# Squared-ReLU MLP of a hybrid decoder step on one core: four inner blocks per down pass, a folded output gate, and stored weight sums

## The chip, the cores and the metric

The kernel runs on one core of one Trainium2 chip. The metric is the device time of one execution in microseconds (us), and the median of the executions shown is what counts. The engines are TensorE (PE; its weight loads are listed as PEld), VectorE (DVE), ScalarE (ACT), GpSimd (POOL) and SyncE (SP), which issues nearly all DMAs.

## The reference, cut to what matters

One inference step of a one-layer decoder runs over 2048 prompt tokens and 32 sample tokens of width 1024: a Mamba-2 group and a sliding-window attention group side by side, an output projection with a residual LayerNorm, then a dense MLP. The change lies in the MLP alone:

```python
h = x * (1.0 + sc_f) + sh_f
u = jnp.square(jax.nn.relu(jnp.einsum('btd,df->btf', h, w_up)))      # 1024 -> 4096
f = jnp.einsum('btf,fd->btd', u, w_down)                            # 4096 -> 1024
x = layer_norm(ALPHA * x + g_f * f, ln2_g, ln2_b)                   # ALPHA = 2 ** 0.25
```

Here `x` is the output of the first LayerNorm, and `g_f` is a row of 1024 gates, one per output column, the same for all prompt tokens.

## The kernel before, in words

Everything is in fp32. A product of two fp32 matrices is made of three fp32r matmuls: each operand is split into a high part (`hi`, an ACT copy to fp32r) and a rest (`lo = src - hi`, a subtraction on DVE or POOL), and `mm3` (L174 to L177) adds hi·hi, hi·lo and lo·hi in PSUM. `split` (L170 to L172) is the helper that makes the two parts.

The MLP walks over the prompt in four quarters `q` of 512 tokens. In each quarter 16 steps `p` stream the same weights again, 256 of the 4096 inner columns at a time (two inner blocks of 128). A step has these parts:

- `w_up` (L1242) loads the 256 columns of w_up as two tiles of 512 KB, `wra` (two buffers) and `wrc` (one buffer), through the SP queue (L1164).
- `w_sums`, by way of `up_ops` (L1167 to L1182), makes the seven weight blocks of a Strassen-Winograd product: DVE forms four sums or differences of half tiles (L1175 `ws`, L1177 `wrc`, L1178 and L1179 `wra`), and the tiles are split into wA, w1, wB and wC. The `lo` parts of wA and wC are made on POOL, those of w1 and wB on DVE (all L1172). These split tiles have one buffer each.
- `up` (L1311) makes seven products of 12 matmuls, each 256 tokens wide (272 in the last quarter, which takes the sample tokens along), in three PSUM tiles `sc`. DVE adds them up straight from PSUM (L1325), squares the ReLU in SBUF (L1339), ACT copies the high part of u (L1341), POOL makes its low part (L1345).
- `w_down` (L1250) loads one block of 128 rows of w_down (`p6` or `p7`, 512 KB, L1252), DVE multiplies it by the gate row into `st2` (L1255, listed as `st<-p,ho`), and `split` gives `wdh` (ACT, L171) and `wdl` (POOL, L172). There are three buffers of each.
- `down` (L1351) runs two such blocks against the two u blocks: for four token tiles `j` and two column halves `n`, 6 matmuls of 512 columns into a PSUM tile (`mm`, three buffers, or `tr`, two). DVE then adds the PSUM tile to the accumulator of that token tile in SBUF (L1374, `p<-mm,p`), which makes 8 additions a step; in the first pass of a quarter ACT copies instead (L1372). The last pass of the last quarter already takes four blocks.

`slot()` (L1267) runs background jobs from a list `bg` at fixed points of a step. `residual(q)` (L1285) fills it: per quarter, rows alpha·ln1_g and alpha·ln1_b are fetched, and each of the four token tiles gets three DVE operations of 128x1024 (L1292 and L1293: xhat times the row, added to the accumulator; L1296: the second row added). At the end of a quarter `h_load` (L1304) fetches and splits the next 512 tokens of h, `finish` (L1403) normalizes, and the results are stored. The sample tokens' down product is kept in one PSUM tile `dec` through the last quarter from raw w_down blocks, and gets its gate and residual in `finish_dec`.

A scheduler orders the instructions of each engine when the program is built; on the chip each engine takes its list in order. SP's list is one queue too: a DMA that waits for its buffer holds back those behind it.

## Time and profile before

| | |
|---|---|
| median of 3 runs | 2650.69 us (2650.53 to 2659.85) |
| the profiled execution: its time | 2660.37 us |
| its span, first to last instruction | 2658.6 us |
| mean granted TensorE clock | 0.965 |
| matmuls / DVE / ACT / POOL instructions | 14231 / 3465 / 1751 / 705 |
| HBM read / written | 253.81 MB / 53.02 MB |

The profiled execution is 9.7 us (0.4%) above the median. The MLP takes the stretch from 967 to 2649 us of the span. A row of a group reads: line, engine, operation, tiles written and read, shapes and count, then busy time in us and mean ns of one, then the idle time of the engine just before those instructions and what ended it. PE's busy time is modelled, since matmuls are pipelined; the distance between the starts of two matmuls shows what one costs in a stream.

### The profile page before, as it was taken

What the parts mean: (1) busy time and instruction counts of PE and PEld (TensorE: products, weight loads), DVE (VectorE), ACT (ScalarE), POOL (GpSimd) and SP (SyncE); (2) the same over time, 40 slices, a digit from 0 to 9 for tenths busy, and PEclk for the clock granted to TensorE, in tenths of its full rate; (3) what the DMA queues carried; (4) which work ended last, traced back from release to release, by engine and by line L of the source; (5) the groups of instructions that cost most, each with busy time, mean ns of one, the idle gap of its engine ahead of it and who ended that gap; (6) DMA issues with size and microseconds to landing.
All of it is one profiled execution on the core that took longest, in us unless ns stands there. A gap on an engine that the chain in (4) does not pass through costs nothing. (4 is left out here: it accounts for less than half of the span.)

```text
span 2658.6 us, 37118 instructions
## 1 busy us (share of the span) xinstructions
PE 2396.3 (90%) x14231; PEld 2015.6 (76%) x14231; DVE 2250.1 (85%) x3465; ACT 958.7 (36%) x1751; POOL 1275.9 (48%) x705
## 2 busy tenths in 40 slices
PE   7899989999999998889978889987889987889997
PEld 5567769878978877778867778876778876777885
DVE  6666677878888779998898998998998899899887
ACT  3544553324345343223234223233223333323332
POOL 4333421332232036556567555567555557546554
PEclk9899999999999999999989999998999998999999
DMA  8654423233154443322223322223332222323221
GB/s 316 235 196 140 132 98 106 62 113 98 60 181 153 172 178 116 107 102 91 94 87 127 111 95 96 88 95 105 102 107 91 96 80 80 119 90 102 80 76 61
DMA packets 111715, 308.23 MB, mean 116 GB/s; under 512 B 15713, under 2 KB 38705, under 8 KB 108385
## 3 DMA queue, kind: packets, MB, share of 16 engines
q1 hardware_dynamic: 106560, 293.78, 32.3%
q10 hardware_dynamic: 4976, 12.07, 1.2%
q8 instruction: 112, 1.84, 0.3%
q14 instruction: 67, 0.54, 0.1%
HBM read 253.81 MB, written 53.02 MB: 115 GB/s over the span
## 5 line engine op out<-in xcount | busy, mean ns | idle before, releaser
L172 POOL TENSOR_TENSOR wdl<-st,wdh 128x1024 fp32r<-128x1024 f32 x127 | 331.2, 2608 | 208.9 <-ACT wdh L171 197.0
L175 PE MATMUL sc<-Hh,wCh 128*128 128x256 f32 (+1 forms) x504 | 158.3, 314 | 127.2 <-DVE U L1325 98.0
L171 ACT ACTIVATE wdh<-st 128x1024 fp32r<-128x1024 f32 x127 | 134.1, 1056 | 293.3 <-DVE st L1255 234.7
L1172 POOL TENSOR_TENSOR wCl<-wrc,wCh 128x1024 fp32r<-128x1024 f32 x63 | 184.5, 2929 | 105.7 <-ACT wCh L1171 97.9
L1255 DVE TENSOR_TENSOR st<-p,ho 128x1024 f32<-128x1024 f32 x128 | 218.3, 1705 | 15.0 <-DMA p<-in_wd 10.4
L1374 DVE TENSOR_TENSOR p<-mm,p 128x512 f32<-128x512 f32 x328 | 217.5, 677 | 5.8 <-PE mm L177 5.8
L175 PEld LDWEIGHTS sc<-Hh,wCh 128*128 128x128 f32 x504 | 102.2, 203 | 153.5 <-DVE U L1325 121.2
L1172 POOL TENSOR_TENSOR wAl<-wra,wAh 128x1024 fp32r<-128x1024 f32 x63 | 166.8, 2648 | 65.5 <-ACT wAh L1171 65.5
L1345 POOL TENSOR_TENSOR B<-c,A 128x512 fp32r<-128x512 f32 x64 | 100.2, 1566 | 139.4 <-ACT A L1341 136.5
L1345 POOL TENSOR_TENSOR u<-c,x 128x512 fp32r<-128x512 f32 x64 | 101.3, 1583 | 134.6 <-ACT x L1341 134.6
L175 PE MATMUL sc<-Hh,wBh 128*128 128x256 f32 (+1 forms) x504 | 149.1, 296 | 16.9 <-DVE c L1325 11.3
L183 POOL TENSOR_TENSOR rs<-ve,mhalf 128x1 f32<-128x1 f32 (+2 forms) x68 | 49.8, 734 | 236.1 <-DVE ve L182 207.1
L175 PE MATMUL mm<-wdh,A 128*128 128x512 f32 x358 | 145.7, 410 | 14.9 <-DVE p L1374 14.7
L1171 ACT ACTIVATE wBh<-wra 128x1024 fp32r<-128x1024 f32 x63 | 66.9, 1061 | 243.0 <-DVE wra L1179 152.5
L1339 DVE SCALAR_TENSOR_TENSOR c<-c 128x512 f32<-128x512 f32 (+1 forms) x128 | 152.0, 1187 | 0.3
L177 PE MATMUL sc<-Hh,wCl 128*128 128x256 f32 (+1 forms) x504 | 150.5, 299 | 0.0
L176 PE MATMUL sc<-Hl,wCh 128*128 128x256 f32 (+1 forms) x504 | 150.4, 298 | 0.0
L177 PE MATMUL sc<-Hh,wBl 128*128 128x256 f32 (+1 forms) x504 | 145.5, 289 | 1.4 <-DVE wBl L1172 1.4
L175 PE MATMUL mm<-wdh,x 128*128 128x512 f32 x352 | 139.8, 403 | 7.8 <-DVE p L1374 7.6
L175 PE MATMUL sc<-Hh,wAh 128*128 128x256 f32 (+1 forms) x504 | 145.7, 289 | 0.8 <-DVE c L1325 0.7
L176 PE MATMUL sc<-Hl,wAh 128*128 128x256 f32 (+1 forms) x504 | 145.1, 288 | 0.4
L176 PE MATMUL sc<-Hl,wBh 128*128 128x256 f32 (+1 forms) x504 | 145.3, 288 | 0.0
(528 smaller groups left out, 8420.7 us busy)
## 6 DMA issues: line engine op xcount, KB each, us to landing
p<-in_wd SPq DMA_DIRECT2D x128, 512.0 KB
wra<-in_wu SPq DMA_DIRECT2D x63, 512.0 KB
...
```

The lines of the kernel that those rows point to most:

```text
L171: S.activation(hi, src, AF.Copy)
L172: (eng or V).tensor_tensor(lo, src, hi.bitcast(F32), ALU.subtract)
L175: PE.matmul(out, lhsT=ahi, rhs=bhi, start=first, stop=False)
L176: PE.matmul(out, lhsT=ahi, rhs=blo, start=False, stop=False)
L177: return PE.matmul(out, lhsT=alo, rhs=bhi, start=False, stop=last)
L183: G.tensor_tensor(r[:P], v[:P], mhalf[:P, 0:n], ALU.pow)
L1171: S.activation(w[0], t, AF.Copy)
L1172: eng.tensor_tensor(w[1], t, w[0].bitcast(F32), ALU.subtract)
L1255: V.tensor_tensor(s2, st, gf, ALU.mult)
L1339: V.scalar_tensor_tensor(c[i][:, :, :N], c[i][:, :, :N], 0.0, c[i][:, :, :N], ALU.max, ALU.mult)
L1345: G.tensor_tensor(h3_(ul), c[i][:, :, 0:256], h3_(uh).bitcast(F32), ALU.subtract)
L1374: V.tensor_tensor(a, mm, a, ALU.add)
```

## The change

The change does five things.

1. **Four blocks per down pass.** The loop is over 8 passes `d` per quarter: two up steps, four `w_down` blocks, one `down` with groups of 12 matmuls. `wdh` and `wdl` get four buffers each, exactly one pass. The accumulators get 8 additions per pass, so per two steps.
2. **The gate is folded into the accumulators.** w_down is split as it was loaded, from `p6`/`p7` themselves, without `st2`. After the seventh pass of a quarter the accumulators are multiplied by the gate row once (`fold`), and the four blocks of the last pass are still multiplied by the gate on DVE.
3. **Weight sums are stored.** In the first quarter the sums that `up_ops` makes are written to DRAM (`sum_d`); later quarters load them and skip the four DVE operations. They then load the first raw tile, three stored pieces and half of the second raw tile: five DMAs, 1.75 MB a step in place of two with 1 MB. Both `wra` buffers are used in every step.
4. **Residual rows are made ahead.** alpha·(xhat·ln1_g + ln1_b) of all 16 token tiles and the sample tokens is made in the background of the first three quarters, two DVE operations a tile, and stored in `xres_d`; `fold` loads it and adds it, one operation.
5. One of the seven up products takes an `mm` tile in place of an `sc` tile; the blocks of the last quarter are loaded into four buffers; the sample tokens' residual and gate are fetched in `finish_dec`.

```diff
+    xres_d = tc.dram_tile([NTOK, DM], F32, name="xres_d")
+    sum_d = tc.dram_tile([16, 128, 4, 512], F32, name="sum_d")
...
         put(wa, ra, G)
-        V.tensor_tensor(s1, rc[:, 0], rc[:, 1], ALU.add)
-        put(w1, s1, V)
-        V.tensor_tensor(rc[:, 0], ra[:, 0], rc[:, 0], ALU.subtract)
-        V.tensor_tensor(ra[:, 0], s1, ra[:, 0], ALU.subtract)
-        V.tensor_tensor(ra[:, 1], ra[:, 1], ra[:, 0], ALU.subtract)
+        if q:
+            ra, s1 = wup[p][2:]
+            put(w1, s1, V)
+        else:
+            V.tensor_tensor(s1, rc[:, 0], rc[:, 1], ALU.add)
+            put(w1, s1, V)
+            V.tensor_tensor(rc[:, 0], ra[:, 0], rc[:, 0], ALU.subtract)
+            V.tensor_tensor(ra[:, 0], s1, ra[:, 0], ALU.subtract)
+            V.tensor_tensor(ra[:, 1], ra[:, 1], ra[:, 0], ALU.subtract)
+            D.dma_start(out=sum_d[p][:, 0], in_=s1)
+            D.dma_start(out=sum_d[p][:, 1], in_=rc[:, 0])
+            D.dma_start(out=sum_d[p][:, 2:4], in_=ra)
         put(wb, ra, V)
         put(wc, rc, G)
...
-    def w_down(f, w=None):
-        st = prt(6 + f % 2)
+    def w_down(f, q, gf=None, w=None):
+        st = prt((6, 7, 4, 5)[f % 4] if q == 3 else 6 + f % 2)
         D.dma_start(out=st, in_=I["wd"][f])
-        hi, lo = w or [wt(1024, "wd" + c, 3) for c in "hl"]
-        s2 = wt(1024, "st2", 1, F32)
-        V.tensor_tensor(s2, st, gf, ALU.mult)
-        split(hi, lo, s2, G)
+        hi, lo = w or [wt(1024, "wd" + c, 4) for c in "hl"]
+        src = st
+        if gf is not None:
+            src = wt(1024, "wra", 2, F32) if q == 3 else st
+            V.tensor_tensor(src, st, gf, ALU.mult)
+        split(hi, lo, src, G)
         return hi, lo, st
...
+    def fold(q, j, gf):
+        r = spare(q, j % 2) if q < 3 else wt(1024, "wra", 2, F32)
+        D.dma_start(out=r, in_=xres_d[128 * tok(q, j):128 * tok(q, j) + 128])
+        V.tensor_tensor(acc[q, j], acc[q, j], gf, ALU.mult)
+        V.tensor_tensor(acc[q, j], acc[q, j], r, ALU.add)
...
-        p5 = prod(1)
+        p5 = prod(1, mm_tile)
...
+        for d in range(8):
+            us, ws = [], []
+            for i in range(2):
+                us.append(step(2 * d + i, q))
+                for f in range(4 * d + 2 * i, 4 * d + 2 * i + 2):
+                    ws.append(w_down(f, q, gf))
...
+            down(q, us, ws, d, dec)
...
+            if d == 6:
+                gf = ada_row(q2("ho"), 5, 128)
+                bg.extend([lambda q=q, j=j, gf=gf: fold(q, j, gf)] for j in range(4))
```

How the lists of the engines change is shown at three places. First DVE's list in a step of the MLP before: `ws`, `wrc` and `wra` (from L1175 and L1177 to L1179) are the weight sums, `st2` the gated block of w_down, `sc` the up products in PSUM, and `p2`, `p3` accumulators.

```order
L1175 TENSOR_TENSOR ws_12456<-wrc_12341 128x512
L1374 TENSOR_TENSOR p3_10276<-tr_12324,p3_10276 128x512
L1177 TENSOR_TENSOR wrc_12341<-wra_12340,wrc_12341 128x512
L1374 TENSOR_TENSOR p3_10276<-tr_12332,p3_10276 128x512
L1325 TENSOR_TENSOR U2_12345<-sc_12363,X1_12344 128x256
L1255 TENSOR_TENSOR st2_12698<-p6_12694,ho_9931 128x1024
L1325 TENSOR_TENSOR c0_12347<-sc_12377,X1_12344 128x256
L1325 TENSOR_TENSOR c0_12347<-sc_12391,U2_12345 128x256
L1172 TENSOR_TENSOR w1l_12460<-ws_12456,w1h_12459 128x512
L1325 TENSOR_TENSOR U3_12346<-sc_12405,U2_12345 128x256
L1178 TENSOR_TENSOR wra_12340<-ws_12456,wra_12340 128x512
```

The same engine in a step of the third quarter of the changed kernel (L1353 is the addition of up products, L1181 a split, L1367 the squared ReLU):

```order
L1353 TENSOR_TENSOR U2_18328<-sc_18346,X1_18327 128x256
L1353 TENSOR_TENSOR c0_18330<-sc_18360,X1_18327 128x256
L1353 TENSOR_TENSOR c0_18330<-mm_18374,U2_18328 128x256
L1353 TENSOR_TENSOR c0_18330<-sc_18403,c0_18330 128x256
L1367 SCALAR_TENSOR_TENSOR c0_18330<-c0_18330 128x2x256
L1181 TENSOR_TENSOR wBl_18443<-wra_18320,wBh_18442 128x1024
L1353 TENSOR_TENSOR U3_18329<-sc_18388,U2_18328 128x256
L1353 TENSOR_TENSOR c1_18331<-mm_18374,U3_18329 128x256
L1353 TENSOR_TENSOR c1_18331<-sc_18417,U3_18329 128x256
L1367 SCALAR_TENSOR_TENSOR c1_18331<-c1_18331 128x2x256
L1402 TENSOR_TENSOR p2_17206<-mm_18466,p2_17206 128x512
L1402 TENSOR_TENSOR p2_17206<-tr_18480,p2_17206 128x512
```

The sums and the gate are gone from the list, and the additions to the accumulators (L1402) now stand together after every second step, eight in a row, where they stood between the up additions in every step. In the whole program DVE has 224 of them in place of 472, 16 gate products of w_down in place of 128, and 16 times the four sums in place of 64 times.

Second POOL's list, two steps of the MLP before. `wdl`, `wAl` and `wCl` are low parts of weight tiles of 128x1024, `u1` and `B2` low parts of u:

```order
L172 TENSOR_TENSOR wdl_15660<-st2_15661,wdh_15659 128x1024
L1172 TENSOR_TENSOR wAl_15630<-wra_15512,wAh_15629 128x1024
L172 TENSOR_TENSOR wdl_15869<-st2_15870,wdh_15868 128x1024
L1345 TENSOR_TENSOR u1_15621<-c0_15519,x1_15620 128x512
L1172 TENSOR_TENSOR wCl_15636<-wrc_15513,wCh_15635 128x1024
L1345 TENSOR_TENSOR u1_15621<-c1_15520,x1_15620 128x512
L172 TENSOR_TENSOR wdl_15877<-st2_15878,wdh_15876 128x1024
L1172 TENSOR_TENSOR wAl_15847<-wra_15729,wAh_15846 128x1024
L172 TENSOR_TENSOR wdl_16086<-st2_16087,wdh_16085 128x1024
L1345 TENSOR_TENSOR B2_15838<-c0_15736,A2_15837 128x512
L1172 TENSOR_TENSOR wCl_15853<-wrc_15730,wCh_15852 128x1024
L1345 TENSOR_TENSOR B2_15838<-c1_15737,A2_15837 128x512
```

Two steps of the changed kernel, the operations of one down pass:

```order
L174 TENSOR_TENSOR wdl_18309<-p6_18306,wdh_18308 128x1024
L174 TENSOR_TENSOR wdl_18315<-p7_18312,wdh_18314 128x1024
L1181 TENSOR_TENSOR wAl_18292<-wra_18165,wAh_18291 128x1024
L174 TENSOR_TENSOR wdl_18457<-p6_18454,wdh_18456 128x1024
L174 TENSOR_TENSOR wdl_18463<-p7_18460,wdh_18462 128x1024
L1181 TENSOR_TENSOR wCl_18297<-wrc_18166,wCh_18296 128x1024
L1373 TENSOR_TENSOR B2_18279<-c0_18177,A2_18278 128x512
L1373 TENSOR_TENSOR B2_18279<-c1_18178,A2_18278 128x512
L1181 TENSOR_TENSOR wAl_18440<-wra_18318,wAh_18439 128x1024
L1373 TENSOR_TENSOR u1_18432<-c0_18330,x1_18431 128x512
L1181 TENSOR_TENSOR wCl_18445<-wrc_18319,wCh_18444 128x1024
L1373 TENSOR_TENSOR u1_18432<-c1_18331,x1_18431 128x512
```

POOL has the same twelve operations, but the four `wdl` now stand together ahead of the two `wCl` and the four parts of u, and they read the loaded blocks `p6` and `p7` themselves, so that a block's buffer is free for the next load only when POOL is done with it.

Third SP's list, the loads of one step of the MLP before:

```order
L1252 DMA p6_15866<-in_wd 128x1024
L1252 DMA p7_15874<-in_wd 128x1024
L1164 DMA wra_15729<-in_wu 128x1024
L1164 DMA wrc_15513<-in_wu 128x1024
L1252 DMA p6_16083<-in_wd 128x1024
```

The loads of a step in a later quarter of the changed kernel:

```order
L1264 DMA ws_18989<-sum_d_69 128x512
L1266 DMA wrc_18727<-sum_d_69 128x512
L1267 DMA wrc_18727<-in_wu 128x512
L1263 DMA wra_18986<-in_wu 128x1024
L1265 DMA wra_18988<-sum_d_69 128x1024
L1266 DMA wrc_18987<-sum_d_69 128x512
L1267 DMA wrc_18987<-in_wu 128x512
L1276 DMA p6_19270<-in_wd 128x1024
L1276 DMA p7_19276<-in_wd 128x1024
```

Five loads of up weights and sums stand where there were two, and the loads of w_down stand behind those of `wrc`, which wait for POOL.

More of the change, by code (lines that the diff above doesn't have):

```diff
@@ L1157, in body, with ws_, w1_ @@
     wup = {}
+    def ws_():
+        return pr2.tile([128, 512], F32, tag="ws", name="ws")
+    def w1_():
+        t = w3(pr2.tile([128, 1024], F32R, tag="w1", name="w1"), 2)
+        return t[:, 0], t[:, 1]
     def w3(t, n):
@@ L1278, in spare, with residuals, row, one @@
         return prt((4 * q + 4 + i) % 6)
-    def row_a(q, j):
-        a = bcast(spare(q, 0), I["rows"][j])
-        S.activation(a, a, AF.Copy, scale=ALPHA)
-        return a
-    def residual(q):
-        a = []
-        bg.append([lambda: a.append(row_a(q, 2))])
-        def mul(j):
-            r = spare(q, 1)
-            D.dma_start(out=r, in_=xhat1_d[128 * tok(q, j):128 * tok(q, j) + 128])
-            V.tensor_tensor(r, r, a[0], ALU.mult)
-            V.tensor_tensor(acc[q, j], acc[q, j], r, ALU.add)
-        def add(j):
-            V.tensor_tensor(acc[q, j], acc[q, j], a[1], ALU.add)
-        for j in range(4):
-            bg.extend([[lambda j=j: mul(j)], [], []])
-        bg.append([lambda: a.append(row_a(q, 3))])
-        for j in range(4):
-            bg.extend([[lambda j=j: add(j)], []])
+    def residuals(q):
+        rows = []
+        def row(t, j):
+            S.activation(bcast(t, I["rows"][j]), t, AF.Copy, scale=ALPHA)
+            rows.append(t)
+        def one(r0, P):
+            r = spare(q, 1)[:P]
+            D.dma_start(out=r, in_=xhat1_d[r0:r0 + P])
+            V.tensor_tensor(r, r, rows[0][:P], ALU.mult)
+            V.tensor_tensor(r, r, rows[1][:P], ALU.add)
+            D.dma_start(out=xres_d[r0:r0 + P], in_=r)
+        bg.append([lambda: (row(q2("ho"), 2), row(spare(q, 0), 3))])
+        for t in range(6 * q, min(6 * q + 6, NTILE)):
+            bg.extend([[lambda t=t: one(128 * t, 128)], [], [], []])
+        if q == 2:
+            bg.append([lambda: one(T, ND)])
+    def fold(q, j, gf):
[3 more added lines that the diff above has]
+        V.tensor_tensor(acc[q, j], acc[q, j], r, ALU.add)
     def h_load(q):
@@ L1349, in body, with down @@
     dnc = [0]
-    def down(q, us, ws, p, dec, after=None):
+    def down(q, us, ws, d, dec, after=None):
         ul_ = [(u[0][:, i], u[1][:, i], u[2][i] if u[2] else None) for u in us for i in range(2)]
@@ L1370, in down @@
                 a = acc[q, j][:, sl]
-                if p == 0:
+                if d == 0:
                     S.activation(a, mm, AF.Copy)
@@ L1408, in finish @@
         ln_out(a, 128, st)
[L1410 to L1417 removed]
     def finish_dec(dec):
[L1420 removed]
+        pt, a, gd = prt(6)[:, 0:512], prt(4)[:32], ada_row(prt(5), 5, ND)[:32]
+        D.dma_start(out=a, in_=xres_d[T:T + ND])
         S.activation(pt, dec, AF.Copy)
[L1422 removed]
         st = p4.tile([128, 2, 6], F32, tag="bst", name="bst", bufs=2)
@@ L1496, in body @@
             dec = tr_tile()
-        us, ws = {0: step(0, q)}, {0: [w_down(0), w_down(1)]}
-        for p in range(15):
-            us[p + 1] = step(p + 1, q)
-            if q == 3 and p == 14:
+        gf = None
+        for d in range(8):
[4 more added lines that the diff above has]
+                    ws.append(w_down(f, q, gf))
+            if d == 7:
                 break
-            if p:
-                ws[p] = [w_down(2 * p), w_down(2 * p + 1)]
-            down(q, [us.pop(p)], ws.pop(p), p, dec)
+            down(q, us, ws, d, dec)
             if q == 0:
                 next(ds, None)
-            if p == 1:
-                bg.extend([] for _ in range(4))
-                residual(q)
-                if q == 3:
-                    bg.extend([[], [dec_res]])
+                next(ds, None)
+            if d == 0 and q < 3:
+                residuals(q)
+            if d == 6:
+                gf = ada_row(q2("ho"), 5, 128)
+                bg.extend([lambda q=q, j=j, gf=gf: fold(q, j, gf)] for j in range(4))
         if q == 3:
             break
-        ws[15] = [w_down(30), w_down(31)]
         h_load(q + 1)
@@ L1521, in body @@
             bg.append(todo)
-        down(q, [us.pop(15)], ws.pop(15), 15, dec)
-    ws[14] = [w_down(28), w_down(29)]
-    ws[15] = [w_down(30), w_down(31, [wt(1024, "wA" + c) for c in "hl"])]
+        down(q, us, ws, 7, dec)
     fin = {}
@@ L1559, in last @@
                 D.dma_start(out=O["y"][1920:2048, sl], in_=a[:, sl])
-    down(3, [us[14], us[15]], ws[14] + ws[15], 14, dec, last)
+    down(3, us, ws, 7, dec, last)
     p4.release()
```

55 lines of the change are left out of this document (26 added, 29 removed).

## The prediction

> **What bounds the kernel now.** I read the stretch of the MLP first, in the table of stretches, whole and then for its second and last quarter.
>
> ```profile
> core 0: us, PE busy (x) PEld busy (x) DVE busy (x) ACT busy (x) POOL busy (x), PEclk, DMA share, GB/s
> 967.00:2649.00 1682.00, 1483.25 (x8591) 1266.40 (x8589) 1539.94 (x1798) 535.06 (x689) 980.88 (x444) 0.96 0.29 97
> 1430.00:1840.00 410.00, 357.07 (x2093) 310.08 (x2092) 383.20 (x437) 132.82 (x169) 245.18 (x112) 0.96 0.30 99
> 2235.00:2640.00 405.00, 372.24 (x2125) 305.81 (x2125) 353.93 (x429) 121.15 (x150) 229.45 (x103) 0.98 0.26 89
> ```
>
> DVE is busy for 1540 of 1682 us (92%), POOL for 58%, the DMA engines for 29%. PE's 88% is modelled, so I asked who waits for whom (1030 to 2640 us).
>
> ```profile
> PE sc L175 <- DVE U L1325: 96.6, 60, 5.1
> PE sc L175 <- DVE c L1325: 38.2, 19, 7.9
> PE mm L175 <- DVE p L1374: 22.4, 20, 4.3
> DVE ws L1175 <- DMA wrc<-in_wu: 42.5, 32, 3.1
> DVE w1l L1172 <- ACT w1h L1171: 24.5, 25, 1.0
> ```
>
> PE waits for DVE; DVE waits for little, and hardly for PE. DVE sets the pace. The timeline shows an undisturbed step, from one `w1l` to the next:
>
> ```profile
> 1300.87 2.48 DVE L1172 TENSOR_TENSOR w1l<-ws,w1h 128x512 fp32r<-128x512 f32 x1 [0.98 <-ACT w1h L1171]
> ...
> 1324.09 2.47 DVE L1172 TENSOR_TENSOR w1l<-ws,w1h 128x512 fp32r<-128x512 f32 x1 [0.98 <-ACT w1h L1171]
> ```
>
> That is 23.2 us a step, 371 us for 16; the quarter of 1682 / 4 = 420 us holds 49 more for residuals, normalization and the next quarter's h. What PE needs at least follows from matmuls without waits between them: ten starts of 256 columns, eight of 512, ten of 272.
>
> ```profile
> 1299.83 0.28 PE L176 MATMUL sc<-Hl,wBh 128*128 128x256 f32 x1
> ...
> 1301.01 0.28 PE L177 MATMUL sc<-Hh,wBl 128*128 128x256 f32 x1
> 1301.13 0.40 PE L176 MATMUL mm<-wdl,A 128*128 128x512 f32 x1
> ...
> 1302.99 0.40 PE L175 MATMUL tr<-wdh,A 128*128 128x512 f32 x1
> ...
> 2400.20 0.29 PE L176 MATMUL sc<-Hl,wAh 128*128 128x272 f32 x1
> ...
> 2401.45 0.29 PE L177 MATMUL sc<-Hh,wAl 128*128 128x272 f32 x1
> ```
>
> So 1.18 / 10 = 0.118 us, 1.86 / 8 = 0.2325 us and 1.25 / 10 = 0.125 us each. The MLP has 64 x 84 up matmuls (1344 of them 272 wide), 64 x 48 down matmuls and the sample tokens' 128:
>
> ```profile
> L1357 PE MATMUL tr<-p,ud 128*32 128x512 f32 x128 | 26.1, 647 | 5.3 <-DVE ud L1344 5.3
> ```
>
> 4032 x 0.118 + 1344 x 0.125 + 3072 x 0.2325 + 26 = 476 + 168 + 714 + 26 = 1384 us. PE's floor is thus 298 us below the stretch; a step's is 84 x 0.118 + 48 x 0.2325 = 21.1 us. More than that the change can't win, since it leaves the matmuls as they are.
>
> **The change part by part.** DVE first.
>
> ```profile
> L1255 DVE TENSOR_TENSOR st<-p,ho 128x1024 f32<-128x1024 f32 x128 | 218.3, 1705 | 15.0 <-DMA p<-in_wd 10.4 <-POOL wdl L172 4.6
> L1374 DVE TENSOR_TENSOR p<-mm,p 128x512 f32<-128x512 f32 x328 | 217.5, 677 | 5.8 <-PE mm L177 5.8
> L1374 DVE TENSOR_TENSOR p<-tr,p 128x512 f32<-128x512 f32 x144 | 95.9, 676 | 0.4 <-PE tr L177 0.4
> L1175 DVE TENSOR_TENSOR ws<-wrc 128x512 f32<-128x512 f32 x63 | 96.9, 1538 | 48.1 <-DMA wrc<-in_wu 48.1
> L1177 DVE TENSOR_TENSOR wrc<-wra,wrc 128x512 f32<-128x512 f32 x63 | 74.5, 1183 | 1.3 <-issue 0.4
> L1178 DVE TENSOR_TENSOR wra<-ws,wra 128x512 f32<-128x512 f32 x63 | 59.5, 945 | 1.9 <-POOL wAl L1172 1.4
> L1179 DVE TENSOR_TENSOR wra<-wra 128x512 f32<-128x512 f32 x63 | 50.6, 803 | 0.1
> L1292 DVE TENSOR_TENSOR p<-p,p 128x1024 f32<-128x1024 f32 x16 | 29.6, 1853 | 10.4 <-DMA p<-xhat_d 10.4
> L1293 DVE TENSOR_TENSOR p<-p,p 128x1024 f32<-128x1024 f32 x16 | 27.0, 1685 | 0.1
> L1296 DVE TENSOR_TENSOR p<-p,p 128x1024 f32<-128x1024 f32 x16 | 30.9, 1935 | 0.2
> ```
>
> Four blocks per pass: 472 additions become 224, 248 x 0.677 = 168 us less. The folded gate: 112 products x 1.705 = 191 us less, 16 of 128 being kept. The stored sums: 48 x (1.538 + 1.183 + 0.945 + 0.803) = 215 us less. The residual: its 48 operations (87.5 us) go; 34 for the rows made ahead and 32 in `fold` come, 66 x about 1.77 (mean of L1292 and L1293) = 117 us. Net: 168 + 191 + 215 + 87.5 - 117 = 545 us less, so DVE falls from 1540 to about 995 us, well below PE's floor.
>
> Those means hold waiting, though. Minimum, median and longest of such operations:
>
> ```profile
> L1172 DVE TENSOR_TENSOR w1l<-ws,w1h x63: 672/2457/2685, 977.2 to 2586.6; 128x512 fp32r<-128x512 f32 x63
> L1255 DVE TENSOR_TENSOR st<-p,ho x128: 1202/1215/3434, 984.4 to 2621.1; 128x1024 f32<-128x1024 f32 x128
> L172 POOL TENSOR_TENSOR wdl<-st,wdh x127: 2373/2406/3926, 987.5 to 2618.7; 128x1024 fp32r<-128x1024 f32 x127
> ```
>
> `w1l` takes 0.67 us alone and 2.46 as a rule: 1.8 us more, most of a POOL operation. The PSUM additions never stretch (0.677). By minima the change takes away 168 + 112 x 1.202 + 192 x 0.67 + 48 x 1.21 - 66 x 1.21 = 409 us, which leaves DVE 1131 us, still below PE. The Trainium skill (SBUF — State Buffer, "SBUF: two separate sides") says that DVE operations with two SBUF inputs and POOL share one pair of ports as an exclusive lock for a whole instruction. The rows agree; by that rule a removed operation's wait can pass to the next one, the smaller sum would hold, and it is the mechanism of the third case below.
>
> POOL keeps its work, per pass of two steps:
>
> ```profile
> L172 POOL TENSOR_TENSOR wdl<-st,wdh 128x1024 fp32r<-128x1024 f32 x127 | 331.2, 2608 | 208.9 <-ACT wdh L171 197.0 <-PE sc L176 11.5
> L1172 POOL TENSOR_TENSOR wCl<-wrc,wCh 128x1024 fp32r<-128x1024 f32 x63 | 184.5, 2929 | 105.7 <-ACT wCh L1171 97.9 <-DMA b<-ada_d 7.8
> L1172 POOL TENSOR_TENSOR wAl<-wra,wAh 128x1024 fp32r<-128x1024 f32 x63 | 166.8, 2648 | 65.5 <-ACT wAh L1171 65.5
> L1345 POOL TENSOR_TENSOR u<-c,x 128x512 fp32r<-128x512 f32 x64 | 101.3, 1583 | 134.6 <-ACT x L1341 134.6
> ```
>
> 4 x 2.61 + 2 x 2.93 + 2 x 2.65 + 4 x 1.58 = 27.9 us of PE's 42.2. But four `wdl` stand together and, with exactly four buffers, start only as a pass ends. From there PE has up work left, about 147 matmuls or 17.3 us by its list, before it needs the first low part of u, and POOL must by then have done four `wdl`, one `wAl`, one `wCl` and that part: 10.4 + 2.65 + 2.93 + 1.6 = 17.6 us. That is a tie; the first splits start some 2 us before the pass ends, so I cost it at nothing, with the serial price in the last rival.
>
> Loads: SP gets three more a step and 0.75 MB more. The nearest row of a load's time is `wrc`, issued and then awaited:
>
> ```profile
> 1312.42 0.33 SPq L1164 DMA_DIRECT2D wrc<-in_wu  x1
> 1315.76 2.14 DVE L1175 TENSOR_TENSOR ws<-wrc 128x512 f32<-128x512 f32 x1 [1.02 <-DMA wrc<-in_wu]
> ```
>
> 3.3 us. 5.5 MB in 42 us are 131 GB/s against 97 now, with the engines at 29%. A single-buffered `wrc` has until the next step's `wCl`, over 10 us away: nothing. Behind it on SP stand the loads of w_down. The third and fourth block of a pass can load only after `wdl` of the first and second, 3.3 + 1.06 us for load and ACT copy, while POOL does another `wdl` and `wAl` (5.3 us): nothing, or 4.4 x 32 = 141 us if uncovered. The stores of sums delay reloads in the first quarter by 0 to 3.3 x 16 = 53 us; I take 0, since the reload waits for `wCl` anyway. `fold` lies in the last two steps of a quarter, ahead of a pass of 22 us; the other PSUM tile and the fetches in `finish_dec` are covered by that pass too.
>
> What is late next is PE. Of the 2.1 us that it loses per undisturbed step (23.2 less 21.1) I keep half: 64 x 1.05 = 67 us. For the start, where PE has no down work to fill in, I add 15, for three changes of quarter 12 each (of the 49 above; a down pass of 22 us now covers the split of h), and for the sums of the first quarter 1 us a step, 16. Estimates all. 1384 + 67 + 15 + 36 + 16 = 1518 us, 164 less than 1682. The span becomes 2658.6 - 164 = 2494.6, the execution (1.8 us more than the span) 2496, and the median, 9.7 us below the profiled one as now, 2487 us.
>
> The Trainium skill (TensorE: Matmul & The Clock Gate, "Back-to-back issue gap") gives N/2.4 + 2.5 ns, 109 and 216 ns for 256 and 512 columns, by which the floor would be about 99 us lower and the median near 2388. The rows show 118 and 232.5 ns, and the measurement decides.
>
> **The rivals.**
>
> PE reaches its floor: only the start stays, 1384 + 15 = 1399, a median near 2368. Against it: even in its best stretch now PE loses 9% of a step.
>
> DVE and POOL still block each other: DVE's PSUM additions queue behind its two-input operations, which queue behind POOL's, and a step stays at 23.2 us; only the work between steps goes. 64 x 23.2 = 1485, plus 26 for the last quarter's sample tokens and 51 for start and changes: 1562, a median of 2531. For it: `w1l`, `wBl` and the squared ReLU all stay. Against it: the longest waits of PE now end with DVE, which loses a quarter to a third of its work.
>
> POOL's burst becomes serial with the passes, and the change is slower: nothing of POOL's chain fits under up work, so a pass costs 22.3 (96 x 0.2325) + 27.9 + 4.4 for the load behind `wdl` = 54.6 us; 32 x 54.6 + 51 = 1798, 116 above now, a median of 2767. It turns slower than now once a pass takes over (1682 - 51) / 32 = 51 us, 8.8 above PE's 42.2. Against it: 147 up matmuls and the two early blocks are free to run meanwhile.
>
> That the scheduler keeps the old work is ruled out by the lists.
>
> **How the numbers follow.** My forecast 0.57 (2440 to 2515), the floor 0.08, the blocked step 0.25 (2515 to 2600), the serial burst 0.07, and 0.03 for a mixture that ends within 0.5% of now, about what a measurement can tell from no change. So faster 0.90, same 0.03, slower 0.07. The range, 2410 to 2595, takes in the forecast, most of the blocked step, and 53 us of uncovered stores; it leaves out the floor and the serial burst.
>
> **What would show it right or wrong.** Right: DVE near 1000 to 1130 us in the MLP, PE's waits on L1325 (now L1353) at under half, a pair of steps at 44 to 45 us, the quarters at about 380 us. `w1l` near 0.7 to 1.5 us would say that the ports are freer, 2.4 that they are not. Wrong: PE waiting for `wdl` or for the low parts of u by several us a pass (the burst), DVE or ACT waiting for `wrc`, `ws` or `p6` and `p7` loads (SP's list), or a step that stays at 23 us with PE still behind L1353.

## The result, and the profile after

| | before | after |
|---|---|---|
| median, us (4 executions each, side by side) | 2655.27 | 2627.47 |
| ratio, with its 95% interval | | 0.990 (0.986 to 0.994) |
| the profiled execution of after: time, span, us | | 2622.87, 2621.1 |

The change makes the kernel 1% faster, 28 us; the forecast was 6%. It lies above the whole range, too. First the table of stretches, for the MLP, its second quarter and the last one:

```profile
967.00:2611.00 1644.00, 1477.15 (x8568) 1272.76 (x8568) 1126.83 (x1267) 527.62 (x680) 984.51 (x441) 0.96 0.43 142
1385.60:1784.40 398.80, 358.58 (x2104) 315.97 (x2102) 275.99 (x293) 134.56 (x172) 254.43 (x112) 0.95 0.47 152
2212.00:2600.00 388.00, 364.13 (x2048) 296.08 (x2047) 223.79 (x274) 107.94 (x137) 197.05 (x92) 0.98 0.33 109
```

DVE (fourth figure) lost 413 us of work in the MLP, 1540 to 1127 us, and the stretch only 38, 1682 to 1644. DVE no longer sets the pace by its total (69%), yet PE still waits for it. The waits of PE from 1030 to 2600 us:

```profile
PE sc L179 <- DVE wBl L1181: 33.4, 18, 5.8
PE sc L177 <- DVE U L1353: 22.6, 19, 3.9
PE mm L179 <- DVE w L1181: 17.7, 8, 5.5
PE sc L177 <- DVE c L1353: 17.3, 14, 3.4
PE sc L177 <- ACT wBh L1180: 16.6, 5, 4.4
PE mm L177 <- DVE p L1402: 9.8, 4, 5.5
```

The waits for the sums from PSUM (L1353) fell from 135 to 40 us, but now the splits of up weights (`wBl`, and `w`, which is w1l) come too late. The group rows of DVE show operations that grew longer (the squared ReLU, `c<-c`, and `wBl`, whose rows of before stand first) or stayed far over their shortest (0.67 us for `w`):

```profile
L1339 DVE SCALAR_TENSOR_TENSOR c<-c 128x512 f32<-128x512 f32 (+1 forms) x128 | 152.0, 1187 | 0.3
L1172 DVE TENSOR_TENSOR wBl<-wra,wBh 128x1024 fp32r<-128x1024 f32 x63 | 121.2, 1923 | 3.0 <-ACT wBh L1171 3.0
...
L1367 DVE SCALAR_TENSOR_TENSOR c<-c 128x512 f32<-128x512 f32 (+1 forms) x128 | 202.6, 1585 | 2.7
L1181 DVE TENSOR_TENSOR wBl<-wra,wBh 128x1024 fp32r<-128x1024 f32 x63 | 134.2, 2130 | 9.9 <-ACT wBh L1180 9.8
L1181 DVE TENSOR_TENSOR w<-ws,w 128x512 fp32r<-128x512 f32 x63 | 98.0, 1555 | 18.9 <-ACT w L1180 18.8
```

An undisturbed pair of steps can be read from every second start of the ACT copy `X`, the first thing that follows a step's first product:

```profile
1627.07 0.38 ACT L1354 ACTIVATE X<-sc 128x256 f32<-128x256 f32 x1 [10.53 <-PE sc L179]
1646.42 0.39 ACT L1354 ACTIVATE X<-sc 128x256 f32<-128x256 f32 x1
1673.17 0.39 ACT L1354 ACTIVATE X<-sc 128x256 f32<-128x256 f32 x1 [10.98 <-PE sc L179]
...
1719.35 0.39 ACT L1354 ACTIVATE X<-sc 128x256 f32<-128x256 f32 x1 [8.48 <-PE sc L179]
```

That is 46.1 us a pair, against 2 x 23.2 = 46.4 before and 42.2 of matmuls. Nothing was won where most of the time is. The timeline of POOL in this pair:

```profile
1635.07 4.78 POOL L174 TENSOR_TENSOR wdl<-p,wdh 128x1024 fp32r<-128x1024 f32 x2 [15.29 <-ACT wdh L173]
1639.79 2.45 POOL L1181 TENSOR_TENSOR wAl<-wra,wAh 128x1024 fp32r<-128x1024 f32 x1
1642.17 5.69 POOL L174 TENSOR_TENSOR wdl<-p,wdh 128x1024 fp32r<-128x1024 f32 x2
1647.83 3.38 POOL L1181 TENSOR_TENSOR wCl<-wrc,wCh 128x1024 fp32r<-128x1024 f32 x1
1651.16 2.99 POOL L1373 TENSOR_TENSOR B<-c,A 128x512 fp32r<-128x512 f32 x2
```

and that of DVE:

```profile
1640.38 2.40 DVE L1181 TENSOR_TENSOR w<-ws,w 128x512 fp32r<-128x512 f32 x1 [0.24 <-ACT w L1180]
...
1644.01 1.60 DVE L1367 SCALAR_TENSOR_TENSOR c<-c 128x512 f32<-128x512 f32 x1
1645.54 3.41 DVE L1181 TENSOR_TENSOR wBl<-wra,wBh 128x1024 fp32r<-128x1024 f32 x1
...
1657.41 0.69 DVE L1367 SCALAR_TENSOR_TENSOR c<-c 128x512 f32<-128x512 f32 x1
1658.02 1.22 DVE L1181 TENSOR_TENSOR wBl<-wra,wBh 128x1024 fp32r<-128x1024 f32 x1
...
1669.58 0.69 DVE L1402 TENSOR_TENSOR p<-tr,p 128x512 f32<-128x512 f32 x1 [8.42 <-PE tr L179]
```

POOL stands idle for 15.3 us until the pass ends, then works 19 us without a pause. While it does, `wBl` takes 3.41 us and the ReLU 1.60; behind it, 1.22 and 0.69. Later DVE itself idles for 8.4 us. PE and the granted clock meanwhile (the clock is the third figure from the end):

```profile
1649.00 0.39 PE L179 MATMUL sc<-Hh,wBl 128*128 128x256 f32 x1 [1.98 <-DVE wBl L1181]
```

```profile
1649.80:1653.40 3.60, 3.60 (x20) 3.60 (x19) 2.38 (x2) 1.38 (x3) 3.60 (x3) 0.53 0.88 241
1653.40:1657.00 3.60, 3.60 (x25) 3.24 (x25) 2.35 (x5) 0.96 (x2) 3.42 (x2) 1.00 0.73 267
```

PE waits 1.98 us, and then the clock is 0.53 for 3.6 us, which costs some 1.5 more (17 matmuls in 3.5 us in place of 2.0). Together that is most of the pair's 3.9 us over its matmuls.

The wait for `wBl` stands at the same place in seven pairs, the fifth to seventh of the second quarter and the fourth to seventh of the third (45.2 to 46.3 us each), and lasts 1.56 to 2.42 us. The low clock does not: it followed in two of the seven, behind 1.98 and 1.73 us, and not behind 2.28 us (at 1603.0) or 2.42 us (at 1951.6). The pair ahead of the one above is as long, 46.3 us, with 2.28 us for `wBl` and 0.68 for the ACT copy `X`; the one behind it, 46.2 us, with 1.58 for `wBl` and 1.4 for L1353, both at a clock of 1.00.

How `wBl` is held up can be read from the lines above. POOL's last two `wdl` end at 1647.86 and `wBl` at 1648.95, 1.09 us later, which is about its length beside an idle POOL. In the whole of after, 33 of the 63 `wBl` took 1.16 to 1.23 us and 30 took 1.95 to 3.46, and every one of these 30 ended 1.08 or 1.09 us behind the end of a POOL operation, however long it took; 45 stretched `w` and 66 stretched ReLUs of 128x512 ended 0.54 to 0.56 us behind one.

### The profile page after: what moved, and what is told of

Its sections match the earlier page's. It is cut to its first block, busy times and chain, and to the rows that moved or that the text cites. A ratio compares the mean times of both kernels' runs of the same rounds, so it can differ in the third digit from the quotient of the medians.

```text
span 2621.1 us, 37177 instructions
## 1 busy us (share of the span) xinstructions
PE 2391.1 (91%) x14231; PEld 2023.8 (77%) x14231; DVE 1836.7 (70%) x2931; ACT 953.7 (36%) x1747; POOL 1282.4 (49%) x703
## 5 line engine op out<-in xcount | busy, mean ns | idle before, releaser
L174 POOL TENSOR_TENSOR wdl<-p,wdh 128x1024 fp32r<-128x1024 f32 x124 | 331.4, 2691 | 383.7 <-ACT wdh L173 383.7
L1402 DVE TENSOR_TENSOR p<-mm,p 128x512 f32<-128x512 f32 x157 | 104.9, 686 | 204.8 <-PE mm L179 204.6
L1181 POOL TENSOR_TENSOR wCl<-wrc,wCh 128x1024 fp32r<-128x1024 f32 x63 | 186.9, 2966 | 67.4 <-ACT wCh L1180 67.3
L173 ACT ACTIVATE wdh<-p 128x1024 fp32r<-128x1024 f32 x124 | 126.7, 1053 | 245.9 <-PE mm L179 135.3
L1181 POOL TENSOR_TENSOR wAl<-wra,wAh 128x1024 fp32r<-128x1024 f32 x63 | 168.2, 2670 | 80.2 <-ACT wAh L1180 73.3
L1367 DVE SCALAR_TENSOR_TENSOR c<-c 128x512 f32<-128x512 f32 (+1 forms) x128 | 202.6, 1585 | 2.7
L177 PE MATMUL sc<-Hh,wCh 128*128 128x256 f32 (+1 forms) x504 | 148.6, 295 | 20.6 <-DVE U L1353 7.5
L179 PE MATMUL sc<-Hh,wAl 128*128 128x256 f32 (+1 forms) x504 | 148.6, 295 | 0.0
L178 PE MATMUL mm<-wdl,x 128*128 128x512 f32 x360 | 145.4, 404 | 0.0
L178 PE MATMUL mm<-wdl,A 128*128 128x512 f32 x360 | 143.7, 399 | 0.0
L179 PE MATMUL mm<-wdh,B 128*128 128x512 f32 x360 | 141.0, 400 | 1.9 <-POOL B L1373 1.9
L1181 DVE TENSOR_TENSOR wBl<-wra,wBh 128x1024 fp32r<-128x1024 f32 x63 | 134.2, 2130 | 9.9 <-ACT wBh L1180 9.8
```

Of the source, the lines that this page charges most:

```text
L173: S.activation(hi, src, AF.Copy)
L174: (eng or V).tensor_tensor(lo, src, hi.bitcast(F32), ALU.subtract)
L177: PE.matmul(out, lhsT=ahi, rhs=bhi, start=first, stop=False)
L178: PE.matmul(out, lhsT=ahi, rhs=blo, start=False, stop=False)
L179: return PE.matmul(out, lhsT=alo, rhs=bhi, start=False, stop=last)
L1181: eng.tensor_tensor(w[1], t, w[0].bitcast(F32), ALU.subtract)
```

## The experiments

The theory from here on: a pass of four blocks puts two up steps back to back and all of POOL's splits of w_down into them (**the burst**), where they stretch DVE's operations with two SBUF inputs. Its rivals: the additional **loads**, or the **background** work (residual rows, fold) in DVE's list. Each row's ratio is to the kernel before, timed beside it; "pair" is an undisturbed one of the first three quarters, from the starts of `X`.

| | kernel | median, us | ratio, 95% interval | pair, us |
|---|---|---|---|---|
| e1 | after, wdl made once | 2511.8 | 0.946 (0.944 to 0.948) | 42.6 |
| e2 | after, wdl on DVE | 2553.3 | 0.962 (0.960 to 0.964) | 44.4 |
| e3 | after, no residual, no fold | 2597.6 | 0.978 (0.976 to 0.980) | 41 to 53, mean 47 |
| e4 | two blocks per pass | 2532.7 | 0.954 (0.952 to 0.956) | 42.3 |
| e5 | e4, three buffers | 2539.0 | 0.956 (0.954 to 0.958) | 42.3 |
| e6 | after, half of wdl on DVE | 2583.5 | 0.972 (0.971 to 0.974) | 39 to 52, uneven |
| e7 | e4, last pass of four | 2528.5 | 0.952 (0.950 to 0.953) | 42.3 |
| e8 | e4, sums made every quarter | 2584.0 | 0.973 (0.972 to 0.975) | 42.3 |
| e9 | after, other product order | 2617.3 | 0.988 (0.986 to 0.989) | 43 to 49 |
| e10 | e7, other product order | 2533.5 | 0.956 (0.954 to 0.958) | 42.3 |
| e11 | after, sums made every quarter | 2669.5 | 1.007 (1.006 to 1.009) | 43 to 54, uneven |
| e12 | after, wdl in halves | 2574.7 | 0.972 (0.970 to 0.974) | 43 to 45 |
| e13 | e7, no split of h | 2486.1 | 0.936 (0.934 to 0.939) | 42.3 |
| e14 | e7, no residual, no fold | 2463.3 | 0.928 (0.926 to 0.930) | 42.3 |
| e15 | e7, no normalization | 2486.5 | 0.936 (0.934 to 0.939) | 42.3 |
| e16 | e7, POOL's splits in halves | 2493.8 | 0.939 (0.937 to 0.942) | 42.3 |
| e17 | e16, loads of xhat ahead | 2493.6 | 0.940 (0.938 to 0.941) | 42.3 |
| e18 | e17, residual rows on POOL | 2499.2 | 0.942 (0.941 to 0.944) | 42.3 |

**e1, wdl made once.**

```diff
-        split(hi, lo, src, G)
+        lo = wlo[f % 4]
+        if q == 0 and f < 4:
+            split(hi, lo, src, G)
+        else:
+            S.activation(hi, src, AF.Copy)
```

> The kernel after, but the low parts wdl of w_down are made only for the first four blocks and then used again for all later ones, so that POOL loses 124 of its splits (2.69 us each, 331 us) and the output is not the reference's. The theory of the burst (four buffers for a pass of four blocks, so POOL stands idle through a pass and then splits four blocks in a row, while DVE's operations with two SBUF inputs are stretched and PE waits for wBl, w1l and the sums) expects a pair of undisturbed steps at 42.5 to 44 us in place of 46.2, wBl at 1.2 to 1.6 us in place of 2.13, the squared ReLU at 1.0 to 1.3 in place of 1.59, and 2520 to 2570 us in all. The theory of the loads (five loads a step through one queue, and stores in the first quarter) expects the pair at 45.5 to 46.5 us and 2605 to 2630 us. The theory of the background (residual rows, fold and gate in DVE's list) expects the same undisturbed pair of about 46 us and about 2600 us or more.

The pair fell to 42.6 us, the time by 116 us: the burst's forecast, and more. `wBl` fell to 1.60 us on average:

```profile
L1181 DVE TENSOR_TENSOR wBl<-wra,wBh 128x1024 fp32r<-128x1024 f32 x63 | 100.5, 1595 | 7.6 <-PE sc L179 4.6 <-ACT wBh L1180 2.9
```

The other two theories are out for the steady pair, with one caution: without `wdl` the raw blocks, too, come free earlier.

**e2, wdl on DVE.**

```diff
-        split(hi, lo, src, G)
+        split(hi, lo, src, V)
```

> The kernel after, with the low parts wdl of w_down made on DVE in place of POOL. The theory of the burst expects that the four splits take 4 x 1.2 = 5 us on DVE in place of 4 x 2.69 = 11 on POOL, that nothing stretches DVE's other operations in the meantime, a pair at 44 to 45.5 us and 2570 to 2610 us. The theory of the loads expects the same pair of 46 to 47 us and 2620 to 2650 us, since the loads stay. The theory of the background, by which DVE's list is too full at some places, expects it slower than after, 2640 to 2700 us, as DVE gets 150 us more.

74 us faster than after although DVE does more, as the burst expects and the background does not. The gain is larger than the burst's case had it (2570 to 2610 us).

**e3, no residual and no fold.**

```diff
-            if d == 0 and q < 3:
-                residuals(q)
...
-                bg.extend([lambda q=q, j=j, gf=gf: fold(q, j, gf)] for j in range(4))
```

> The kernel after without the residual of the prompt tokens: neither the rows made ahead nor the fold (product with the gate, addition of the residual) at the end of a quarter are there, so DVE loses 66 operations of 128x1024 and the queue their loads and stores; the gate stays on the last four blocks, and the output is not the reference's. The theory of the background expects the changes of quarter to fall from 65 to 74 us a pair to 52 to 58 and the first quarter's pairs to 47 to 50, and 2540 to 2580 us in all. The theory of the burst expects 66 x 1.2 to 1.8 us at most in part uncovered, the undisturbed pair unchanged at 46, and 2590 to 2615 us. The theory of the loads expects 2600 to 2620 us.

30 us: what the burst expected of it in time, though the pairs became uneven. The changes of quarter stayed (72.4 and 47.6 us for the first one's two pairs).

**e4, two blocks per pass**, each step's up ahead of the pass of the step before, in place of the loop over `d`:

```diff
+        for p in range(16):
...
+            us[p] = step(p, q)
+            ws[p] = [w_down(f, q, gf if p > 13 else None) for f in (2 * p, 2 * p + 1)]
...
+            down(q, [us.pop(p - 1)], ws.pop(p - 1), p - 1, dec)
```

> The kernel after with part 1 alone undone: two blocks per down pass, 8 accumulator additions a step again (about 248 more on DVE, 168 us), each step's up products ahead of the pass of the step before, while the four buffers of wdh and wdl are kept, so that two passes fit and splits can start while a pass runs. The fold, the stored sums and the rows made ahead stay. The theory of the burst expects that POOL's splits spread out, wdl no longer waits for the end of a pass (384 us of such idle time falls under 150), 44 to 45.5 us for two steps, and 2560 to 2600 us, although DVE has more to do. The theory of the loads expects no gain (2620 to 2650 us), and so does that of the background, by which 168 us more on DVE cost (2650 to 2700 us).

95 us faster than after, with the 248 additions back on DVE, and more than the burst's case had it (2560 to 2600 us). POOL's idle time ahead of `wdl` fell less than forecast, from 380 to 258 us (967 to 2600 us) and not under 150. Its steps, again from `X`:

```profile
1579.11 0.39 ACT L1354 ACTIVATE X<-sc 128x256 f32<-128x256 f32 x1 [0.17 <-PE sc L179]
1600.30 0.38 ACT L1354 ACTIVATE X<-sc 128x256 f32<-128x256 f32 x1 [0.16 <-PE sc L179]
1621.45 0.39 ACT L1354 ACTIVATE X<-sc 128x256 f32<-128x256 f32 x1 [0.17 <-PE sc L179]
```

42.3 us a pair is PE's floor to within 0.1 us. Its POOL and DVE show why:

```profile
1599.27 4.75 POOL L174 TENSOR_TENSOR wdl<-p,wdh 128x1024 fp32r<-128x1024 f32 x2 [5.01 <-ACT wdh L173]
1604.16 2.43 POOL L1181 TENSOR_TENSOR wAl<-wra,wAh 128x1024 fp32r<-128x1024 f32 x1
1609.84 2.63 POOL L1181 TENSOR_TENSOR wCl<-wrc,wCh 128x1024 fp32r<-128x1024 f32 x1 [3.25 <-ACT wCh L1180]
```

```profile
1608.36 0.69 DVE L1367 SCALAR_TENSOR_TENSOR c<-c 128x512 f32<-128x512 f32 x1
1608.97 1.22 DVE L1181 TENSOR_TENSOR wBl<-wra,wBh 128x1024 fp32r<-128x1024 f32 x1
```

With only two `wdl` in a row POOL is idle from 1606.6 to 1609.8, and that is when `wBl` runs, in 1.22 us. In the pass of four the other two `wdl` stand in this hole.

**e5, three buffers.**

```diff
...
-        hi, lo = w or [wt(1024, "wd" + c, 4) for c in "hl"]
+        hi, lo = w or [wt(1024, "wd" + c, 3) for c in "hl"]
...
```

> The kernel of two blocks per pass (2533 us) with three buffers of wdh and wdl in place of four, as in the kernel before; the fourth block of the last pass takes the tiles of wA, and the two splits of a step stand behind the up products of the next step, as before. It asks whether the fourth buffer or the shorter pass brought the 95 us. If it is the buffers (splits can start only while one is free), a pair of undisturbed steps goes from 42.3 to 44 or more and the time to 2570 to 2620 us. If the shorter pass itself is enough, since POOL's splits then come in groups of two, the pair stays at 42.3 to 43 us and the time at 2525 to 2550 us.

The pair stays at 42.3, so my thought that the fourth buffer had mattered falls: the shorter pass is enough.

**e6, half of wdl on DVE.**

```diff
-        split(hi, lo, src, G)
+        split(hi, lo, src, V if f % 2 else G)
```

> The kernel after, with four blocks per pass, and every second low part wdl made on DVE: the burst is two POOL splits and two DVE splits side by side. If the burst's length on POOL (11 us ahead of wAl, wCl and the low parts of u) is what costs, halving it gives most of it: a pair of 43.5 to 45 us in place of 46.2, and 2545 to 2580 us. If it is that any split on POOL stretches DVE's operations with two SBUF inputs, the splits that run side by side on DVE and POOL stretch one another (DVE's wdl at 2.4 us in place of 1.5), the pair stays at 45 to 46 us, and the time at 2590 to 2625 us, worse than with all four on DVE (2553 us).

Between the two: the time lies 3.5 us above the range of the first case and 6.5 below that of the second. The group of `wdl` on DVE in e2 and then in e6:

```profile
L174 DVE TENSOR_TENSOR wdl<-p,wdh 128x1024 fp32r<-128x1024 f32 x124 | 189.4, 1532 | 49.2 <-ACT wdh L173 48.5
```

```profile
L174 DVE TENSOR_TENSOR wdl<-p,wdh 128x1024 fp32r<-128x1024 f32 x61 | 125.2, 2052 | 28.1 <-ACT wdh L173 28.1
```

It took 2.05 us in place of 1.53, and the time is 30 us worse than with all of them there. DVE's half is held up beside POOL's; POOL's own half is not, at 2.64 us against 2.69 in after.

**e7, last pass of four**: `down(q, [us[14], us[15]], ws[14] + ws[15], 14, dec)` in every quarter.

> The kernel of two blocks per pass and four buffers, with the last two passes of every quarter put together into one of four blocks, so that 22 us of matmuls in place of 11 stand beside the split of the next quarter's h, the fold and the normalization. If the changes of quarter are what is left over the floor (three changes of 110 to 120 us for the last and the first pair together, against 84.4 us of matmuls), each falls by about 8 us, and the time to 2500 to 2515 us. If the burst of four splits comes back at these places and takes it again, the time stays at 2525 to 2545 us.

4 us, and the intervals overlap: not shown to gain anything.

**e8, sums made in every quarter.** `up_ops` without `if q`, `w_up` always as in the first quarter, nothing stored.

> The kernel of two blocks per pass and four buffers with part 3 undone: the weight sums are made in every quarter again, by four operations on DVE, and two tiles are loaded a step in place of five pieces; nothing of the sums is stored. DVE gets 48 x 4.5 = 215 us more by the means before (130 us by minima), 75 MB fewer are moved. If DVE's work still sets the pace once the burst is gone, the time is 2580 to 2630 us, a pair of 44 to 46 us. If DVE has room and the loads of sums cost something in the steady step, it is 2515 to 2540 us and the pair stays at 42.3 us.

51 us slower than e4, and yet the pair stays at 42.3: in the steady step DVE has room and the loads cost nothing. Part 3 pays where work piles up: 42 of the 54 us between the two profiled executions lie in the first two pairs of the last three quarters (43 and 60 us in e8 against 31 and 54 in e4, in the second quarter). Neither expectation had that. The bytes that go are some 54 MB and not 75 (HBM read and written together, 378.7 MB in e4 and 324.1 in e8).

**e9 and e10, another product order**, on the four-block pass and on e7. The sums change order with their products; the number of operations does not.

```diff
-        add(u2, prod(2), x1)
-        add(cb(0, 0), prod(3), x1)
-        p5 = prod(1, mm_tile)
-        add(cb(0, 1), p5, u2)
...
+        add(cb(0, 0), prod(3), x1)
+        add(u2, prod(2), x1)
+        add(cb(0, 1), prod(5), u2)
+        p5 = prod(1, mm_tile)
```

> The kernel after, four blocks per pass, with the seven up products in another order: 0, 3, 2, 5, 1, 4, 6 in place of 0, 2, 3, 1, 4, 5, 6. The split blocks of wB (products 2 and 5) have one buffer; in the order of after they are read last by the sixth product of a step and first by the second of the next, so that in two steps back to back 24 matmuls (2.8 us) lie between, in which ACT makes wBh (1.06 us) and DVE wBl (1.2 us alone, up to 3.4 behind POOL's splits). In the new order five products, 60 matmuls or 7.1 us, lie between. POOL's burst and the number of operations stay. If this short distance is what turns the burst into a wait of PE, the pair falls from 46.2 to 42.5 to 44 us, PE's waits for wBl from 33 to under 10 us, and the time to 2530 to 2580 us. If the burst costs by its total work in the up phase, another operation of DVE is late in place of wBl, the pair stays at 45 to 46.5 and the time at 2605 to 2630 us.

> The kernel with two blocks per pass, four buffers and a last pass of four (2529 us), with the up products in the order 0, 3, 2, 5, 1, 4, 6. Its steady pair is at 42.3 us, PE's own time, so the order can save something only at the changes of quarter, where two steps stand back to back. If the distance of wB matters there, 2505 to 2520 us; if not, 2520 to 2535 us.

In e9 PE's waits for `wBl` are gone, and others have come in their place:

```profile
PE sc L177 <- DVE c L1353: 45.2, 21, 8.4
PE mm L179 <- DVE w L1181: 31.5, 17, 5.0
```

10 us at most were won, and the intervals of e9 and after overlap, so it isn't the one late operation but all of DVE's work in that place. In e10 nothing was gained.

**e11, sums made in every quarter, four blocks.** As e8, on after.

> The kernel after, four blocks per pass, with the weight sums made in every quarter again on DVE and nothing stored or loaded of them. Under two blocks per pass this cost 51 us. If DVE's work in the up phase is what paces the four-block pass, it costs more here: each step gets four more operations in the up phase (about 3.5 us), PE waits for wBl behind them, a pair of 49 to 52 us, and 2690 to 2760 us, slower than the kernel before. If the four-block pass is paced by POOL's burst or by the loads alone, it costs 50 us or less: 2640 to 2680 us by the burst, 2600 to 2630 us by the loads.

0.7% slower than the kernel before: without part 3 the change would be a loss. 42 us is what part 3 gives here, as little as the burst's case had it.

**e12, wdl in halves.**

```diff
-        split(hi, lo, src, G)
+        S.activation(hi, src, AF.Copy)
+        for n in range(2):
+            sl = slice(512 * n, 512 * n + 512)
+            G.tensor_tensor(lo[:, sl], src[:, sl], hi[:, sl].bitcast(F32), ALU.subtract)
```

> The kernel after, with each wdl split on POOL issued as two operations of 128x512 in place of one of 128x1024, so 124 more operations on POOL and the same bytes. If an operation of POOL keeps DVE's two-input operations out for its whole length, DVE gets in between the halves: w1l, wBl and the squared ReLU get shorter (wBl 1.6 to 1.9 in place of 2.13 us), the pair falls to 44 to 45.5, and the time to 2590 to 2615 us. If the two engines only share a rate, nothing shortens and POOL's fixed cost is added: 2620 to 2650 us.

53 us faster than after, more than either case had it, although POOL's `wdl` take 388 us in place of 329. Its groups:

```profile
L1285 POOL TENSOR_TENSOR wdl<-p,wdh 128x512 fp32r<-128x512 f32 x248 | 387.7, 1594 | 340.9 <-ACT wdh L1282 336.4 <-DMA sum_d<-wra 4.2
L1181 DVE TENSOR_TENSOR wBl<-wra,wBh 128x1024 fp32r<-128x1024 f32 x63 | 130.7, 2075 | 16.5 <-ACT wBh L1180 16.5
```

The gain speaks for an operation of POOL holding DVE out for its whole length. But the mean of `wBl` hardly fell (2.13 to 2.08 us; ReLU of 128x512 1.63 to 1.55; `w` 1.56 to 1.48), and the scheduler made other lists, so how much of the 53 us is the shorter hold stays open.

**e13, e14 and e15: the works at a change of quarter, left out one by one.** `h_load(q + 1)`; `residuals(q)` and `fold`, as in e3; `finish(q, j)`.

> The kernel of two blocks per pass with a last pass of four (2529 us), without the load and split of the next quarter's h: every quarter multiplies the first quarter's h again, so the output is not the reference's. The last and first pair of two quarters take 107 to 117 us there, against 84.4 of matmuls. If the chain of loads, sums and splits of h is what PE waits for at a change (H has one buffer, so it can start only when the last up product is done), each change falls by 15 to 25 us and the time to 2455 to 2485 us. If DVE's list (residual, fold, normalization) is the cause, it falls by 10 us in all or less.

> The same kernel of two blocks (2529 us) without residual rows and fold, as in the third experiment; the output is not the reference's. In the four-block pass this gave 30 us. If these operations cost by standing in DVE's list ahead of the up phase, the gain is smaller where DVE has room: 2505 to 2525 us. If they cost by their waits for loads of xhat (DVE waited 28 to 37 us for them), the gain is the same or more, 2480 to 2505 us, and the second and third pair of the quarters fall from 50 to 54 us towards 43 to 46.

> The same kernel of two blocks (2529 us) without the normalization of the first three quarters' results, which are stored as they stand, so the output is not the reference's. It takes 24 statistics, 12 scalings on ACT, 12 products on DVE and 12 additions on POOL out of the first two steps of a quarter. If the normalization is what makes the second pair of a quarter 53 us, it falls to 43 to 46 us, and the time to 2490 to 2510 us; if not, 2520 to 2530 us.

42, 65 and 42 us. Each costs, none is the one cause; e13 ends 1 us short of its first case, and e14 and e15 gave more than expected of them. In e14 the second pair of the first three quarters is 39 to 43 us in place of 53 to 54. All of it stands in one list; that of DVE at the second change of quarter in after:

```profile
1719.70:1769.80 50.10, 41.63 (x230) 37.09 (x229) 49.38 (x43) 18.54 (x25) 32.92 (x14) 0.90 0.51 168
```

DVE is busy for 49.4 of 50.1 us with fold, gate, splits of weights, sums of h and two up steps.

**e16, POOL's splits in halves, two blocks**: as e12, for wdl, wAl and wCl.

> The same kernel of two blocks (2529 us), with all of POOL's splits of weights (wdl, wAl, wCl) issued as two operations of half the size. In the four-block pass halving wdl alone gave 53 us. Its steady pair is PE's own time already, so only the changes of quarter can gain: 2505 to 2522 us if DVE's operations stand behind long POOL operations there, 2525 to 2545 us if not, POOL's fixed cost being added.

35 us, more than expected. Of the 33 us between the profiled executions, 22 lie in the last and first pairs at the changes of quarter, 15 of them at the second change alone, and 5.5 ahead of the first `X`. The squared ReLU of 128x512 took 1.02 us on average in place of 1.23 in e7, `w` 1.20 in place of 1.70, but `wBl` 1.70 in place of 1.61. At 2494 us, 6.1% faster than before, it is with e17 the best version of the whole computation. The table of stretches for its MLP, which is 127 us shorter than that of after:

```profile
967.00:2484.00 1517.00, 1428.12 (x8562) 1245.13 (x8560) 1121.58 (x1489) 526.49 (x674) 1061.17 (x694) 0.98 0.47 153
```

**e17 and e18: what the residual rows cost.** The load is issued two slots ahead; then the rows' operations go to POOL.

```diff
-            bg.extend([[lambda t=t: one(128 * t, 128)], [], [], []])
+            bg.extend([[lambda t=t: load(128 * t, 128)], [], [lambda t=t: one(128 * t, 128)], []])
...
```

> The kernel of two blocks with POOL's splits in halves (2494 us), and the loads of xhat for the residual rows issued two background slots ahead of the operations that use them; the output is the reference's. If DVE's idling behind these loads is what the residual rows cost, DVE's waits for xhat fall from 24 us to under 6, the second pairs of the first three quarters fall from 51 to 57 us to 46 to 50, and the time to 2465 to 2482 us. If it is the time of the operations, 2485 to 2500 us.

> The same with the 34 operations of the residual rows on POOL (as 66 of half a tile and 2 for the sample tokens' two halves each, some 100 us on POOL) in place of DVE. If their time on DVE is the cost, 2455 to 2480 us; if POOL's list becomes late in the pairs where they stand, or they stretch DVE's operations as before, 2485 to 2520 us.

e17 says nothing on its question. The tile has one buffer, so that the load still stands behind the store of the rows before it, and DVE waits as in e16, where it was 23.7 us:

```profile
DVE p L1329 <- DMA p<-xhat_d: 24.9, 11, 3.9
```

e18 is no faster either, as its second case had it, though DVE is rid of the rows' operations. Whether the waits or the operations make up the 65 us of e14, or the fold, which e14 leaves out too and e17 and e18 keep, stays open.

## Why the prediction was wrong, point by point

**The change part by part, as measured.** e8 has parts 2, 4 and 5 and the fourth buffers of part 1, without the long pass: 71 us less than before. Part 3 brings 51 more (e8 to e4). Part 1 takes 95 back (e4 to after). The part that I credited with 168 us of DVE's work is the one that loses.

**DVE's saving: close to the smaller sum, in part by luck.** 413 us went, where the minima said 409 and the means 545. By rows, the operations that went or came make 537 us. Those that stayed take 67 us more, the squared ReLU 51 and `wBl` 13, with `w` 16 less: that much of the waiting passed on to others, as the prediction had named it. The other 58 us are a matter of counting: the records of neighbouring DVE operations overlap by some 0.07 us (the ReLU above ends at 1645.61, `wBl` starts at 1645.54), which the busy time of a stretch counts once and a sum of means twice.

**"That is a tie ... so I cost it at nothing": the step that failed.** The reckoning asked only when the low part of u would be late, POOL's 17.6 us against PE's 17.3. That DVE's two-input operations stand in the same microseconds, and are held up there, it had in a rival and not in the sum. What came late was `wBl`, by 1.56 to 2.42 us in each of the seven pairs, and behind it came a low clock or further waits.

**"Of the 2.1 us that it loses per undisturbed step I keep half": nothing was saved.** The steady loss is (46.1 - 42.2) x 32 = 125 us in place of 67.

**Start and changes: "15 ... 12 each ... 16", 67 us in all: too small by half.** The stretch less floor and steady loss, 1644 - 1384 - 125, leaves 135. Before it was 1682 - 1384 - 32 x 4.2 = 164 by the same sum, so I had expected 97 us to go, and 29 went. The down pass of 22 us was to cover the split of h, yet fold, gate and that split stand in DVE's list together with the two up steps. The two errors, 58 and 68 us, are 1644 - 1518 = 126. The other 14 us lie between the profiled executions and the medians: 9.7 us above it for before, 4.6 below it for after.

**The first quarter's stores and the loads: at nothing in the prediction, and shown to be nothing under two blocks alone.** e8, which has neither, is no faster in its first quarter, 397 us from `X` to `X` against 394 in e4. Under four blocks the first quarter takes 417 us with the stores (after) and 410 without (e11), and 407 in the kernel before.

**The signs.** Two of the signs of being right came, DVE at 1127 us and PE's waits on L1353 at 40 of 135, and yet the pair stayed at 46.1 us. They speak of DVE's total and of one wait of PE; another wait took its place.

**The rivals.** "DVE and POOL still block each other" had the blocking, with 0.25, and its step of 23.2 us (23.1 measured). That the step agrees is in part luck: it let PE wait behind the PSUM additions, and PE waited for the splits of weights. Its price of 2531 us was too low since it let the work between the steps go for 51 us. The serial burst of POOL alone, slower than before, did not come: PE hardly waited for `wdl` or the low parts of u.

**Which half of the mechanism.** That POOL's `wdl` in the up phase costs the pair is shown (e1, e2, e4 against after, and 1.22 against 3.41 us in one timeline). That POOL holds DVE's two-input operations out for whole operations of its own is what the ends show, 1.08 or 1.09 us behind a POOL operation for each stretched `wBl` of after; e4 and e12, with other lists, show the same 1.08 to 1.09 us (18 and 44 of 63). The Trainium skill (SBUF — State Buffer, "SBUF: two separate sides") calls this an exclusive lock that is held for the whole instruction, and the traces agree. Open is how much of the gain of e6, e12 and e16 is the hold and how much the scheduler's other lists, and what each work at a change of quarter costs in after itself.
